# Two blocks in one launch: the steps of S5, its loads and its gate are placed differently, and two norms get idle matmuls

## The chip, the cores and the metric

The kernel runs on one core of one Trainium2 chip. What counts is the time of one execution on the device, in microseconds; the median over runs is given.

## The reference

A sequence of 256 tokens with 2048 features in fp32 goes through two different transformer blocks. What the change touches:

```
first block:   xn = rmsnorm(h);  z = xn @ w_in        -> q, k, v, o, gates, u
               hm = mlstm(q, k, v, gates)             4 heads of 256, chunks of 128 tokens
               ys = s5_groups(u, ...)                 64 groups of 16 channels, state 64 (complex),
                                                      then per group a gated linear unit (s5_glu_w)
               h  = h + concat[hm, ys] @ w_out
               h  = h + peer(rmsnorm(h))              8 heads choose among experts peer_u, peer_v
               x  = rmsnorm(h)
second block:  h = rms_norm(x) * (1 + scale1) + shift1;   x = x + gate1 * mixing_sublayer(h)   (w_in_2, w_out_2)
               h = rms_norm(x) * (1 + scale2) + shift2;   x = x + gate2 * swiglu(h)            (w_ffn_in, w_ffn_out)
```

S5 is a linear recurrence per group. The kernel computes it in pieces of 8 tokens: "taps" are the direct products within a piece, "in" gives each piece's contribution to the state, the recurrence over the 32 pieces gives the states, and "out" adds taps and states to the output. Gelu and the gated linear unit follow.

## The kernel before

All large products run on TensorE as three matmuls per piece of K: an fp32 weight is split into a high and a low part (ScalarE copies it rounded, L247, VectorE subtracts, L248), the activations have been split before (xh, xl), and L274 to L276 multiply high by low, high by high and low by high. A weight chunk (`raw`, 512 KB, loaded by SyncE at L238) holds two pieces of K of 128 rows for 512 columns, so that it is 12 matmuls: two pieces, two halves of the tokens, three products. Four split buffers and four `raw` buffers stand. A tile of 512 columns accumulates in two banks `g` (psG has four), and its callback copies them out.

Everything beside the projections is written as generators in queues (`side`). `gemm` calls `step` after each weight chunk, and `step` advances the first generator of each queue by n steps. The Tile framework then orders the instructions of each engine from the order in which they were traced and from its own simulated times, so that the place of a step in the program sets its rank; it may move ahead or fall back on its engine.

The second half of `w_in` in phase_a has eight tiles of eight chunks, 64 chunks, at two steps per chunk: v, q, k and o of heads 0 and 1, then the same of heads 2 and 3. Beside it run, in queue 0, `s5_all`: put_u (5 steps), taps(1), in(0), taps(2), in(1), taps(3), in(2), in(3) (37 steps), states (15), and for each quarter q out(q) (6), and for q-1 move and gate (8, of which 6 are empty). In queue 1 and 2 run the gates and the heads of the mLSTM; heads 0 and 1 are added when k(2), the third tile, is done (chunk 24). taps(0) runs earlier, in the first half of `w_in`.

Transposes, S5's products and the heads' products take banks `b` of psS, four in all. `in(q)` is a chain of transposes (L308), copies on ScalarE, matmuls (L518), a copy and transposes again. The recurrence (L540 to L543) is 31 times four operations on GpSimd, in order. `out(q)` needs the taps out of DRAM (Kd, L554, tile `s5t0`, one buffer), builds a matrix on VectorE (L563 ff.), multiplies (L576, L582), transposes and applies Gelu. The move (L599, L603) stores the quarter to DRAM in eight pieces and loads it back turned; the gate (L610) multiplies it and puts it into `ys`. When all four are done, `ys` is split (L849, L850) for the second half of w_out's K, which runs first; then `hm`, the heads' output, is transposed and split for the first half.

The q and k tiles are copied by ScalarE (`ev`, L813, two buffers), transposed into banks `b` and convolved. v goes to V1 (L806, one buffer), which heads 0 and 1 hold until they are done; heads 2 and 3 use it next. The output gate `og` has one buffer too.

The first norm (`final_norm` and `norm_T`) stands between the expert products of `peer` (L1115 to L1117) and the second block's `w_in`: the last products' sums are added and transposed (`put_Y`, L308 into banks `g`), the root is found (`rC`, L301), transposed to a row (L308), and VectorE and ScalarE make xh and xl (L346, L348). The second norm is the same between `w_out_2` and `w_ffn_in`.

Of the kernel before, what the change touches and what calls it, by code (L numbers as in the profile page):

```python
# [24 lines left out]
T = 256  # L25
# [125 lines left out]
class Kern:  # L151
    def __init__(self, tc, A, ctx):
        self.tc, self.nc, self.A, self.ctx = tc, tc.nc, A, ctx
        self.side = [[], [], []]
        self.GB, self.heads = {}, set()
        self.raw_slots, self.raw_n = [None], 0
        self.half_step = []

    def pool(self, name, bufs=1, space=None):
# [10 lines left out]
    def step(self, n=1):  # L170
        for q in self.side:
            for _ in range(n):
                while q:
                    try:
                        next(q[0])
                        break
                    except StopIteration:
                        q.pop(0)
# [147 lines left out]
    def norm_r(self, work, ss, name="rstd"):  # L326
# [3 lines left out]
        return self.rstd(work, st, D, name)  # L330

    def put_Y(self, YT, Y, k0, bank=None):

        for k in range(0, Y[0].shape[-1] // 128, 2):
            p = self.transpose4([Y[tb][:, (k + i) * 128:(k + i + 1) * 128] for i in range(2) for tb in range(2)], bank)
            self.nc.scalar.activation(YT[:, k0 + k:k0 + k + 2].rearrange("p k t -> p (k t)"), p, AF.Copy)

    def norm_T(self, YT, r, xh, xl, work, gain, shift):

        nc, V = self.nc, self.nc.vector  # L340
        b = self.transpose4([r[:, tb:tb + 1].to_broadcast([128, 128]) for tb in range(2)])
        row = work.tile([128, T], F32, name="nrow")
        nc.scalar.activation(row, b[:, :T], AF.Copy)
        for k in range(KD):
            v = work.tile([128, T], F32, name="nv", bufs=4)
            V.scalar_tensor_tensor(v, YT[:, k], gain[:, k:k + 1], row, op0=OP.mult, op1=OP.mult)  # L346
            nc.scalar.activation(xh[:, k], v, AF.Identity, bias=shift[:, k:k + 1])
            V.scalar_tensor_tensor(xl[:, k], v, shift[:, k:k + 1], xh[:, k].bitcast(F32), op0=OP.add, op1=OP.subtract)  # L348


    def s5_params(self, p):
        nc = self.nc
        prm = p.tile([128, 96 + 2048], F32, name="s5prm")
        nc.sync.dma_start(prm, self.A["s5p"])
        lre, lim, ldt = (prm[:, i * 32:(i + 1) * 32] for i in range(3))
# [87 lines left out]
    def s5_taps(self, p, q):  # L443
# [37 lines left out]
        dr = self.pb.tile([128, 16, 16], F32, name="t", bufs=3)  # L481
        nc.sync.dma_start(dr.rearrange("p g o -> p (g o)"), self.A["s5d"][:, q * 256:(q + 1) * 256])
        nc.gpsimd.tensor_tensor(dr, dr, self.ident[:, None, :16].to_broadcast([128, 16, 16]), op=OP.mult)
# [47 lines left out]
    def s5_states(self, p):  # L531
# [5 lines left out]
        for c in range(31):  # L537
# [6 lines left out]
            if c % 2:  # L544
                yield

    def s5_out(self, p, q, yg):

        nc, V, q5 = self.nc, self.nc.vector, self.s5
        pw, pn, cn, U, S = q5["pw"], q5["pn"], q5["cn"], self.U[q], self.S  # L550
        ms = slice(8 * q, 8 * q + 8)
        t0 = p.tile([128, 8, 16, 16], F32, name="s5t0")
        k = self.Kd
        nc.sync.dma_start(t0.rearrange("p i g o -> p (i g o)"),  # L554
                            bass.AP(tensor=k.tensor, offset=k.offset + q * 16 * 3840,
                                    ap=[[256, 8], [3840, 16], [1, 2048]]))

# [12 lines left out]
        for hf in range(2):  # L570
# [7 lines left out]
            for a in range(2):  # L578
                for r in range(2):
                    for gr in range(4):  # L580
# [4 lines left out]
                                         tile_position=(hf * 64, gr * 32))  # L585
            nc.scalar.activation(YS[:, hf * 256:(hf + 1) * 256], b[:, :256], AF.Copy)
        yield
        b = self.transpose4([YS[:, i * 128:(i + 1) * 128] for i in range(4)])
        nc.scalar.activation(yg[:, 16 * q:16 * q + 16].rearrange("p g c -> p (g c)"), b, AF.Gelu)
        yield  # L590

    def s5_glu(self, p, q, yg, ys):

        nc, V = self.nc, self.nc.vector
        if q == 0:
# [7 lines left out]
        nc.sync.dma_start(yT, yd[2 * q:2 * q + 2].rearrange("n p x -> p n x"))  # L603
        for _ in range(6):
            yield
        for hf in range(2):
            gt = hf * 4 + q
            b = self.bank()
            for s in range(2):
                nc.tensor.matmul(b[:, s * 256:(s + 1) * 256], self.glu[:, gt, s, :], yT[:, hf],  # L610
                                 start=s == 0, stop=s == 1, skip_group_check=True)
            sg = self.pb.tile([128, 256], F32, name="t", bufs=3)
# [5 lines left out]
    def s5_all(self, p, uT, ys):  # L618
        yield from self.s5_put_u(p, uT)
        self.glu = p.tile([128, 8, 2, 128], F32, name="s5c")  # L620
        self.nc.sync.dma_start(self.glu.rearrange("p a b c -> p (a b c)"), self.A["glu"])
        for q in range(4):
            if q < 3:
                yield from self.s5_taps(p, q + 1)
            yield from self.s5_in(p, q)
        yield from self.s5_states(p)
        yg = self.xx.tile([128, 64, 32], F32, name="X1")
        for q in range(4):
            yield from self.s5_out(p, q, yg)
            if q:  # L630
                yield from self.s5_glu(p, q - 1, yg, ys)
        yield from self.s5_glu(p, 3, yg, ys)

# [112 lines left out]
    def phase_a(self):  # L746
        nc, V, A = self.nc, self.nc.vector, self.A
        with ExitStack() as ex:
# [19 lines left out]
            bg = mp.tile([128, 8], F32, name="bg")  # L768
            nc.sync.dma_start(bg, A["b_gates"])
            self.add_side(self.s5_params(s5))  # L770
# [69 lines left out]
            for tb in range(2):  # L840
                nc.sync.dma_start(X[tb], A["x"][tb * 128:(tb + 1) * 128, :])
            xh = self.act.tile([128, KD, T], F32R, name="xh")
            xl = self.act.tile([128, KD, T], F32R, name="xl")
            mix = [[s5.tile([128, 8, T], F32R, name=n, bufs=2 if n == "s5q" else 1) for n in nn]
                   for nn in (("s5q", "s5q"), ("s5t0", "s5b"))]
            for q in range(4):
                k, y = slice(2 * q, 2 * q + 2), ys[:, 2 * q:2 * q + 2]
                h, l = (z[:, k] for z in mix[1])
                nc.scalar.activation(h, y, AF.Copy)  # L849
                V.tensor_tensor(l, y, h.bitcast(F32), op=OP.subtract)  # L850

# [236 lines left out]
    def peer_v(self, p, AT, half, slots, steps=1):  # L1088
# [44 lines left out]
        for hf in range(2):  # L1133
# [4 lines left out]
            self.step(4 * steps)  # L1138
        more.close()
        self.drain()  # L1140
        return P

    def peer(self, xh, xl, r):
# [37 lines left out]
        def final_norm():  # L1181
# [4 lines left out]
            for n in range(4):  # L1186
                s = slice(n * 512, (n + 1) * 512)
                Y = [p.tile([128, 512], F32, name="fy", bufs=4) for _ in range(2)]
                for tb in range(2):
# [3 lines left out]
                    for z, j in ((x, 0), (Y[tb], 1)):  # L1193
# [4 lines left out]
                        else:  # L1198
                            nc.scalar.activation(sq, z, AF.Square, accum_out=ss[:, j, tb, n:n + 1])
                self.put_Y(YT, Y, 4 * n, self.bank_g)  # L1200
            st = p.tile([128, 2, 2], F32, name="fst")
            V.tensor_reduce(st.rearrange("p a b -> p (a b)"), ss.rearrange("p a b n -> p (a b) n"), axis=AX.X, op=OP.add)
# [329 lines left out]
    def phase_c(self, p, get_x):  # L1532
# [3 lines left out]
        with ExitStack() as ex2:  # L1536
# [3 lines left out]
            xl = self.act.tile([128, KD, T], F32R, name="xl")  # L1540
            self.norm_T(YT, r2, xh, xl, p, gain, shift)
            self.keep.close()
# [130 lines left out]
            with tp(name="po", bufs=1) as p:  # L1673
# [13 lines left out]
                def cb_o(i, P):  # L1687
# [7 lines left out]
                    self.put_Y(YT, [X[tb][:, s] for tb in range(2)], s.start // 128)  # L1695
                self.gemm("w_out_2", LAST, KD, yh, yl, cb_o)
                xh = self.act.tile([128, KD, T], F32R, name="xh")
                xl = self.act.tile([128, KD, T], F32R, name="xl")
                self.norm_T(YT, self.norm_r(p, ss), xh, xl, p, gain, shift)
                for tb in range(2):  # L1700
# [56 lines left out]
```

## Time and profile before

| | us |
|---|---|
| median of 3 runs | 3672.2 (3669.62 to 3672.81) |
| profiled execution | 3670.36 |
| its span, first to last instruction | 3668.6 |
| TensorE busy | 3570.9 (97%) |
| VectorE busy | 2722.6 (74%) |
| ScalarE busy | 2006.5 (55%) |
| GpSimd busy | 542.9 (15%) |
| mean granted TensorE clock | 0.991 |

TensorE is PE in the rows, VectorE DVE, ScalarE ACT, GpSimd POOL, SyncE SP. Matmuls are pipelined, so that the starts of successive ones lie closer than each lasts. The clock is the share of full speed that was granted; its two levels are 1.2 and 2.4 GHz.

### The profile page before, as it was taken

What the parts mean: (1) busy time and instruction counts of PE and PEld (TensorE: products, weight loads), DVE (VectorE), ACT (ScalarE), POOL (GpSimd) and SP (SyncE); (2) the same over time, 40 slices, a digit from 0 to 9 for tenths busy, and PEclk for the clock granted to TensorE, in tenths of its full rate; (3) what the DMA queues carried; (4) which work ended last, traced back from release to release, by engine and by line L of the source; (5) the groups of instructions that cost most, each with busy time, mean ns of one, the idle gap of its engine ahead of it and who ended that gap; (6) DMA issues with size and microseconds to landing.
All of it is one profiled execution on the core that took longest, in us unless ns stands there. A gap on an engine that the chain in (4) does not pass through costs nothing. (4 is left out here: it accounts for less than half of the span.)

```text
span 3668.6 us, 52912 instructions
## 1 busy us (share of the span) xinstructions
PE 3570.9 (97%) x17442; PEld 2957.3 (81%) x17442; DVE 2722.6 (74%) x5631; ACT 2006.5 (55%) x3511; POOL 542.9 (15%) x669
## 2 busy tenths in 40 slices
PE   9997999999999999999999999999999999999999
PEld 7776887788888788887888788888887888888888
DVE  8685779759999977777777878765777666666554
ACT  5555655555555455555555665765455555555443
POOL 1060002204455500001000101000111000000000
PEclk9998999999999999999999999999999999999999
DMA  7656555555555578888887554566886577777665
GB/s 207 185 161 152 186 176 161 167 183 175 171 166 173 166 248 285 288 284 312 290 285 262 180 157 135 160 202 196 281 292 224 165 228 227 235 224 218 189 196 161
DMA packets 228515, 766.07 MB, mean 209 GB/s; under 512 B 40528, under 2 KB 44496, under 8 KB 226192
## 3 DMA queue, kind: packets, MB, share of 16 engines
q1 hardware_dynamic: 197728, 647.89, 56.0%
q0 software_dynamic: 30512, 114.81, 9.9%
q8 instruction: 137, 2.24, 0.2%
q14 instruction: 138, 1.13, 0.1%
HBM read 753.23 MB, written 9.37 MB: 208 GB/s over the span
## 5 line engine op out<-in xcount | busy, mean ns | idle before, releaser
L247 ACT ACTIVATE wh<-raw 128x512 fp32r<-128x512 f32 (+2 forms) x2068 | 1287.9, 628 | 1285.8 <-PE g L275 638.3
L248 DVE TENSOR_TENSOR wl<-raw,wh 128x512 fp32r<-128x512 f32 (+2 forms) x2068 | 1453.8, 713 | 670.3 <-ACT wh L247 621.0
L274 PE MATMUL g<-wh,xl 128*128 128x512 f32 (+2 forms) x3296 | 1271.6, 386 | 14.4 <-ACT wh L247 9.2
L275 PE MATMUL g<-wh,xh 128*128 128x512 f32 (+2 forms) x3296 | 1265.4, 384 | 0.0
L276 PE MATMUL g<-wl,xh 128*128 128x512 f32 (+2 forms) x3296 | 1096.7, 387 | 27.4 <-DVE wl L248 27.3
L276 PEld LDWEIGHTS g<-wl,xh 128*128 128x128 f32 x3296 | 611.7, 189 | 152.8 <-DVE wl L248 41.4
L274 PEld LDWEIGHTS g<-wh,xl 128*128 128x128 f32 x3296 | 623.7, 189 | 136.1 <-ACT wh L247 10.9
L275 PEld LDWEIGHTS g<-wh,xh 128*128 128x128 f32 x3296 | 623.5, 189 | 118.0 <-issue 0.4
L1115 PE MATMUL g<-wh,uev 128*128 128x512 f32 x504 | 196.5, 390 | 3.7 <-ACT wh L247 2.2
L1115 PE MATMUL b<-wh,uev 128*128 128x512 f32 x504 | 196.2, 389 | 0.0
L1116 PE MATMUL g<-wh,uev 128*128 128x512 f32 x504 | 196.1, 389 | 0.0
L1116 PE MATMUL b<-wh,uev 128*128 128x512 f32 x504 | 196.1, 389 | 0.0
L248 DVE TENSOR_TENSOR wl<-xh,wh 128x512 fp32r<-128x512 f32 x202 | 135.3, 688 | 68.7 <-ACT wh L247 27.9
L1057 POOL TENSOR_TENSOR e<-e,t 128x256 fp32r<-128x256 f32 x128 | 131.0, 1027 | 367.6 <-DVE e L1056 272.4
L247 ACT ACTIVATE wh<-xh 128x512 fp32r<-128x512 f32 x202 | 127.6, 632 | 51.6 <-PE g L1116 38.3
L274 PE MATMUL g<-wh,fl 128*128 128x512 f32 (+1 forms) x440 | 154.4, 351 | 0.0
L275 PE MATMUL g<-wh,fh 128*128 128x512 f32 (+1 forms) x440 | 154.2, 351 | 0.0
L910 POOL DMA_DIRECT2D xl<-in_w_ada x116 | 61.2, 528 | 595.2 <-DVE xl L906 585.8
L1117 PE MATMUL g<-wl,uev 128*128 128x512 f32 x504 | 147.5, 389 | 0.9 <-DVE wl L248 0.9
L906 DVE SCALAR_TENSOR_TENSOR xl<-xl 128x1024 f32<-128x1024 f32 x116 | 141.5, 1220 | 8.2 <-DMA xl<-in_w_ada 8.2
L1117 PE MATMUL b<-wl,uev 128*128 128x512 f32 x504 | 146.9, 390 | 0.0
L276 PE MATMUL g<-wl,fh 128*128 128x512 f32 (+1 forms) x440 | 132.6, 348 | 0.0
(558 smaller groups left out, 4111.6 us busy)
## 6 DMA issues: line engine op xcount, KB each, us to landing
raw<-in_peer_u SPq DMA_DIRECT2D x256, 512.0 KB, 3.6
raw<-in_w_in SPq DMA_DIRECT2D x192, 512.0 KB, 3.6
raw<-in_w_ffn_in SPq DMA_DIRECT2D x176, 512.0 KB, 4.2
raw<-in_peer_v SPq DMA_DIRECT2D x130, 512.0 KB, 5.6
xl<-in_w_ada POOLq DMA_DIRECT2D x116, 512.0 KB, 5.9
xh<-in_peer_v SPq DMA_DIRECT2D x101, 512.0 KB, 5.3
raw<-in_w_ffn_out SPq DMA_DIRECT2D x88, 512.0 KB, 4.1
raw<-in_w_out SPq DMA_DIRECT2D x64, 512.0 KB, 4.1
```

Of the source, the lines that this page charges most:

```text
L247: nc.scalar.activation(h[:, :n], r, AF.Copy)
L248: nc.vector.tensor_tensor(l[:, :n], r, h[:, :n].bitcast(F32), op=OP.subtract)
L274: nc.tensor.matmul(o, xl[:, k - ka, t], hs, start=k == ka, stop=False)
L275: nc.tensor.matmul(o, xh[:, k - ka, t], hs, start=False, stop=False)
L276: nc.tensor.matmul(o, xh[:, k - ka, t], ls, start=False, stop=k == kb - 1)
L906: self.tc.keep_in_program_order(nc.vector.scalar_tensor_tensor(r, r, 1.0, cr, op0=OP.mult, op1=OP.mult, accum_out=self.macc[:, 2 * m + hf: ...
L910: nc.gpsimd.dma_start(r, w[n * 128:(n + 1) * 128, cs])
L1057: E.tensor_tensor(o2[:, :, 1], f(o2[:, :, 0]), bc(f(self.wl), t), op=OP.mult)
L1115: nc.tensor.matmul(o, w[:, 1, t], h, start=i1 == 0, stop=False)
L1116: nc.tensor.matmul(o, w[:, 0, t], h, start=False, stop=False)
L1117: nc.tensor.matmul(o, w[:, 0, t], l, start=False, stop=i1 == 127)
```

## The change

While S5's taps and inputs run, queue 0 advances three steps per chunk instead of two (`dense`). The load of the taps for a quarter is issued at the end of the quarter before, ahead of its transposes (`s5_load`), and for the first quarter ahead of the states. The move of quarter q comes right behind out(q), and its gate behind out(q+1) with no empty steps between; its matmuls are kept in the order of the program. The split of `ys` for w_out moves into `s5_all`: quarters 0 to 2 ahead of ten empty steps and the last gate, quarter 3 behind it. The loads of S5's parameters, of its diagonal and of the gate bias go from SyncE's queue to GpSimd's. Matmuls whose result is never read (`fill`) are put in: 10 each after the last two quarters of `final_norm`, 8 in its `norm_T`, 16 after `w_out_2` and 8 in the `norm_T` that follows.

```diff
 def step(self, n=1):
         for q in self.side:
-            for _ in range(n):
+            for _ in range(n + (self.dense if q is self.side[0] else 0)):
...
+    def fill(self, l, r, n):
+
+        b = self.bank()
+        for _ in range(n):
+            self.nc.tensor.matmul(b, l, r, start=True, stop=True)
...
-    def norm_T(self, YT, r, xh, xl, work, gain, shift):
+    def norm_T(self, YT, r, xh, xl, work, gain, shift, fill):
...
         nc.scalar.activation(row, b[:, :T], AF.Copy)
+        fill()
...
-        nc.sync.dma_start(prm, self.A["s5p"])
+        nc.gpsimd.dma_start(prm, self.A["s5p"])
...
-        nc.sync.dma_start(dr.rearrange("p g o -> p (g o)"), self.A["s5d"][:, q * 256:(q + 1) * 256])
+        nc.gpsimd.dma_start(dr.rearrange("p g o -> p (g o)"), self.A["s5d"][:, q * 256:(q + 1) * 256])
...
+    def s5_load(self, p, q):
+
+        self.t0 = p.tile([128, 8, 16, 16], F32, name="s5t0")
+        k = self.Kd
+        self.nc.sync.dma_start(self.t0.rearrange("p i g o -> p (i g o)"),
+                               bass.AP(tensor=k.tensor, offset=k.offset + q * 16 * 3840,
+                                       ap=[[256, 8], [3840, 16], [1, 2048]]))
...
     def s5_out(self, p, q, yg):
...
+        t0 = self.t0
...
+        if q < 3:
+            self.s5_load(p, q + 1)
         yield
         b = self.transpose4([YS[:, i * 128:(i + 1) * 128] for i in range(4)])
...
-    def s5_glu(self, p, q, yg, ys):
+    def s5_move(self, q, yg):
...
         nc.sync.dma_start(yT, yd[2 * q:2 * q + 2].rearrange("n p x -> p n x"))
-        for _ in range(6):
-            yield
+        return yT
+
+    def s5_glu(self, q, yT, ys):
...
-                nc.tensor.matmul(b[:, s * 256:(s + 1) * 256], self.glu[:, gt, s, :], yT[:, hf],
-                                 start=s == 0, stop=s == 1, skip_group_check=True)
+                self.tc.keep_in_program_order(
+                    nc.tensor.matmul(b[:, s * 256:(s + 1) * 256], self.glu[:, gt, s, :], yT[:, hf],
+                                     start=s == 0, stop=s == 1, skip_group_check=True))
...
+        self.dense = 1
         for q in range(4):
             if q < 3:
                 yield from self.s5_taps(p, q + 1)
             yield from self.s5_in(p, q)
+        self.dense = 0
+        self.s5_load(p, 0)
         yield from self.s5_states(p)
         yg = self.xx.tile([128, 64, 32], F32, name="X1")
+        yT = None
         for q in range(4):
             yield from self.s5_out(p, q, yg)
             if q:
-                yield from self.s5_glu(p, q - 1, yg, ys)
-        yield from self.s5_glu(p, 3, yg, ys)
+                yield from self.s5_glu(q - 1, yT, ys)
+            yT = self.s5_move(q, yg)
+        self.mix_s5(p, ys, (0, 1, 2))
+        for _ in range(10):
+            yield
+        yield from self.s5_glu(3, yT, ys)
+        self.mix_s5(p, ys, (3,))
+
+    def mix_s5(self, p, ys, qs):
+
+        if qs[0] == 0:
+            self.ysh, self.ysl = (p.tile([128, 8, T], F32R, name=n) for n in ("s5t0", "s5b"))
+        for k in [4 * hf + q for hf in range(2) for q in qs]:
+            self.nc.scalar.activation(self.ysh[:, k], ys[:, k], AF.Copy)
+            self.nc.vector.tensor_tensor(self.ysl[:, k], ys[:, k], self.ysh[:, k].bitcast(F32), op=OP.subtract)
...
-            nc.sync.dma_start(bg, A["b_gates"])
+            nc.gpsimd.dma_start(bg, A["b_gates"])
...
+        self.filler = ws[127][:, 0, 0:128], ws[127].rearrange("p a t -> p (a t)")
         self.drain()
         return P
...
                 self.put_Y(YT, Y, 4 * n, self.bank_g)
+                if n > 1:
+                    self.fill(*self.filler, 10)
...
-            self.norm_T(YT, r2, xh, xl, p, gain, shift)
+            self.norm_T(YT, r2, xh, xl, p, gain, shift, lambda: self.fill(*self.filler, 8))
...
                 self.gemm("w_out_2", LAST, KD, yh, yl, cb_o)
+                filler = p.tile([128, 512], F32R, name="fill")
+                nc.scalar.activation(filler, yh[:, 0:2], AF.Copy)
+                self.fill(filler[:, 0:128], filler, 16)
...
-                self.norm_T(YT, self.norm_r(p, ss), xh, xl, p, gain, shift)
+                self.norm_T(YT, self.norm_r(p, ss), xh, xl, p, gain, shift,
+                            lambda: self.fill(filler[:, 0:128], filler, 8))
```

## Rows read from the trace of the kernel before

**Rows 1.** Busy time by stage: stretch, us, busy and instructions of each engine, clock, DMA share, GB/s.
```profile
277.00:351.00 74.00, 55.03 (x448) 42.14 (x448) 42.22 (x75) 39.14 (x63) 0.00 (x0) 0.82 0.65 155
351.00:397.00 46.00, 46.00 (x213) 37.76 (x212) 33.30 (x105) 24.27 (x52) 0.00 (x0) 1.00 0.50 155
...
2041.00:2058.00 17.00, 9.95 (x39) 7.43 (x38) 15.29 (x46) 10.82 (x25) 1.14 (x2) 0.70 0.50 186
...
2913.50:2928.00 14.50, 7.89 (x24) 5.62 (x23) 12.22 (x38) 8.06 (x19) 0.00 (x0) 0.65 0.20 69
...
sum 3668.60, PE 3570.87 PEld 2957.33 DVE 2722.56 ACT 2006.51 POOL 542.93; mean PE 357.09 PEld 295.73 DVE 272.26 ACT 200.65 POOL 54.29
```

**Rows 2.** Timeline of TensorE, 277 to 351 us; in brackets the idle time before and its releaser.
```profile
321.40 0.65 PE L576 MATMUL b<-s5t,X 128*32 128x128 f32 x16 [3.13 <-DMA s5t<-Kd]
...
330.52 3.53 PE L610 MATMUL b<-e,s5c 128*128 128x256 f32 x8 [3.38 <-DMA e<-yd]
...
345.01 0.79 PE L274 MATMUL g<-wh,s5b 128*128 128x512 f32 x1 [4.50 <-DVE s5b L850]
```

**Rows 3.** Busy time and count of L274 on TensorE from the span's start to three times.
```profile
0.00:129.10 129.10, 57.37 (x160) 0.97 0.72 207
0.00:199.50 199.50, 88.60 (x238) 0.98 0.67 192
...
0.00:267.40 267.40, 120.88 (x320) 0.99 0.64 185
```

**Rows 4.** Timeline of TensorE, transposes and S5 output matmuls that use banks b.
```profile
146.84 0.60 PE L308 MATMUL b<-ident,e 128*128 128x128 f32 x4
147.27 1.04 PE L308 MATMUL b<-ident,ev 128*128 128x128 f32 x8
...
199.63 0.60 PE L308 MATMUL b<-ident,e 128*128 128x128 f32 x4
200.07 1.04 PE L308 MATMUL b<-ident,ev 128*128 128x128 f32 x8
...
267.51 0.64 PE L576 MATMUL b<-s5t,X 128*32 128x128 f32 x16
```

**Rows 5.** Timeline of GpSimd: the first and the last operation of the recurrence that waited or ended.
```profile
202.87 0.32 POOL L542 TENSOR_TENSOR s5t<-s5t,X 128x64 f32<-128x64 f32 x1 [51.32 <-DVE X L528]
...
267.34 0.72 POOL L543 TENSOR_TENSOR s5b<-s5t,s5t 128x64 f32<-128x64 f32 x1
```

**Rows 6.** Timeline of TensorE, matmuls of 512 columns at full clock; three lie between.
```profile
92.15 0.39 PE L275 MATMUL g<-wh,xh 128*128 128x512 f32 x1
...
93.06 0.39 PE L276 MATMUL g<-wl,xh 128*128 128x512 f32 x1
```

**Rows 7.** SyncE's issues of two lines: count, ns min/median/max, first and last start.
```profile
L554 SPq DMA_DIRECT2D s5t<-Kd x4: 604/627/648, 156.9 to 306.9; - x4
...
L599 SPq DMA_DIRECT2D yd<-X x32: 302/448/3194, 279.0 to 333.4; - x32
```

**Rows 8.** Timeline of TensorE at the first norm.
```profile
2029.42 0.71 PE L308 MATMUL g<-ident,AT 128*128 128x128 f32 x5
...
2040.72 1.58 PE L308 MATMUL g<-ident,AT 128*128 128x128 f32 x13
...
2051.32 0.79 PE L274 MATMUL g<-wh,xl 128*128 128x512 f32 x1 [2.58 <-DVE xl L348]
```

**Rows 9.** Timeline of TensorE at the second norm.
```profile
2918.78 0.66 PE L308 MATMUL b<-ident,rstd 128*128 128x128 f32 x2 [2.51 <-DVE rstd L301]
...
2922.01 0.80 PE L274 MATMUL g<-wh,xl 128*128 128x512 f32 x1 [2.58 <-DVE xl L348]
```

**Rows 10.** Timeline of TensorE where the first half of w_out ends.
```profile
397.52 1.47 PE L308 MATMUL b<-ident,hm 128*128 128x128 f32 x12
```

**Rows 11.** Timeline of ScalarE, two copies out of the projection's accumulators.
```profile
128.94 0.69 ACT L813 ACTIVATE ev<-g,rA 128x512 f32<-128x512 f32 x1 [0.28 <-PE g L276]
...
266.75 1.27 ACT L806 ACTIVATE V<-g,rA 128x512 f32<-128x512 f32 x2 [0.27 <-PE b L723]
```

More of the change, by code (lines that the diff above doesn't have):

```diff
@@ L551, in s5_out @@
         ms = slice(8 * q, 8 * q + 8)
[L552 to L556, printed above, removed]
+        t0 = self.t0
         G2 = p.tile([128, 2, 8, 8, 16], F32, name="s5q", bufs=2)
@@ L590, in s5_out @@
         yield
-    def s5_glu(self, p, q, yg, ys):
-        nc, V = self.nc, self.nc.vector
+    def s5_move(self, q, yg):
+        nc = self.nc
         if q == 0:
@@ L603, in s5_glu @@
         nc.sync.dma_start(yT, yd[2 * q:2 * q + 2].rearrange("n p x -> p n x"))
-        for _ in range(6):
-            yield
+        return yT
+    def s5_glu(self, q, yT, ys):
+        nc, V = self.nc, self.nc.vector
         for hf in range(2):
@@ L625, in s5_all @@
             yield from self.s5_in(p, q)
+        self.dense = 0
+        self.s5_load(p, 0)
         yield from self.s5_states(p)
         yg = self.xx.tile([128, 64, 32], F32, name="X1")
+        yT = None
         for q in range(4):
@@ L843, in phase_a @@
             xl = self.act.tile([128, KD, T], F32R, name="xl")
[L844 to L850, printed above, removed]
+            mix = [[s5.tile([128, 8, T], F32R, name="s5q", bufs=2) for _ in range(2)], [self.ysh, self.ysl]]
             def mix_hm():
```

## The prediction

> **What bounds the kernel now.** I read the busy shares by stage first. TensorE is busy 3570.87 of 3668.60 us [rows 1], so the sum of all its gaps is 97.7 us, and an edit can only win where TensorE stands still or runs below full clock. Three of the stages there have such gaps and are touched by the diff. From 277 to 351 us TensorE is busy 55.03 of 74.00 us, so 18.97 us are idle, and its granted clock is 0.82; that it lies between the two levels means that it spent part of the stretch at 1.2 GHz, and 55.03 x (1 - 0.82) = 9.9 us is what that costs. From 2041 to 2058 (the first norm) it is busy 9.95 of 17 at 0.70, and from 2913.5 to 2928 (the second) 7.89 of 14.5 at 0.65. The stretch right behind the first, 351 to 397, is full: 46.00 of 46.00 us at 1.00.
>
> Next I read TensorE's timeline of 277 to 351. Seven waits make up the 18.97 us; [rows 2] has three of the larger ones. All belong to S5: its output matmuls (L576), its gate (L610), and the first w_out product, which waits 4.50 us for the split of S5's result (L850).. So S5's tail is late, and the projection's matmuls have run out by then.
>
> Why it is late is seen by following S5 back. Counting L274 on TensorE [rows 3] (four per weight chunk, 96 before the second half of w_in) shows that at 129.1 us 16 chunks were done, at 199.5 us 35.5, at 267.4 us 56. The last input transposes run just then, at 199.63 us [rows 4], although the generator puts them at chunk 21.5. The recurrence on GpSimd starts 3 us later and runs until 268.06 us, 65 us in all [rows 5], and out(0) follows at 267.51 [rows 4]. Behind it come four times out, move, gate.
>
> **The change part by part.** A chunk is 12 matmuls; four at full clock take 93.06 - 92.15 = 0.91 us [rows 6], so one is 0.2275 us and a chunk 2.73 us.
>
> *Three steps per chunk.* Taps 1 to 3 and the four inputs are 37 steps: 18.5 chunks at two per chunk, 12.3 at three. The recurrence is placed 6.2 chunks earlier, or 16.8 us. That is the upper bound of the gain. The lower bound is nothing: S5 runs 14 chunks behind its place already (35.5 against 21.5), since each of its TensorE groups waits for a copy of the one before and products that are ready go ahead meanwhile. Neither end fits by itself: being traced earlier gives each step an earlier turn, but does not shorten a round trip. I take the middle, 8.4 us.
>
> *What such a gain is worth.* Nothing of the tail disappears; what moves 8.4 us earlier are its waits, and products still to do fill them. Idle 18.97 and clock 9.9 make 28.8 us that could be won at most, so 8.4 fits within it. The recurrence's own 65 us stay.
>
> *Move and gate, taps a quarter ahead.* The load of Kd (L554) was issued for the last time at 306.9 us [rows 7], after the last L576 of the quarter before, and out(3) starts at 321.40 after waiting 3.13 us for it [rows 2]. The new place in the program is earlier, but the buffer is single: the load still cannot start before that L576 has read it, and SP issues it as soon as it has. I cost it at nothing, with a gain of 3.13 us as the upper bound. The move (8 stores of yd and a reload) is traced one out earlier and the gate loses its six empty steps. The stores are 32 of 0.448 us [rows 7]; nine issues a quarter are some 4 us of SP, and weight loads queue behind them. They began at 279.0 us, right behind out(0), so SP runs them by readiness already and their place changes nothing. The reload's wait of 3.38 us [rows 2] is the bound on either side: out's work covers it or the next one has it. The pin keeps the gate's matmuls behind the instruction traced before them; they run later than their place already, so nothing. The splits of quarters 0 to 2 come ahead of the last gate, so two of eight pairs remain behind it; the 4.50 us of the last wait [rows 2] bound the gain, and I leave it in the 8.4. Queued behind a late gate on TensorE are the transposes of q and k of the second half, and behind them heads 2 and 3.
>
> *Loads moved from SP to GpSimd* (the S5 parameters, four diagonals, the gate bias): six DMAs of the same bytes. Taps and inputs end before the recurrence, and GpSimd stood idle for 51.32 us ahead of it [rows 5]; that is the cover, and I cost the move at nothing. Without it, one issue costs 0.63 us of a queue (L554 in [rows 7]), six 3.8.
>
> *Idle matmuls at the first norm.* 10 after each of n = 2 and 3, 8 in the norm: 28 x 0.2275 = 6.4 us of TensorE. Full clock in 2041 to 2058 would give 9.95 x 0.30 = 3.0 us. Against it, the transposes of the output are run among the products as soon as they are ready, from 2029.42 us [rows 8], 11 us before the last ones at 2040.72. Fills that follow in the program can be put there as well, and 20 of them delay the products by up to 4.5 us. The 8 others (1.8 us) fit into the 2.58 us ahead of the first product at 2051.32 [rows 8]. Gain 3.0, loss 4.5; the rows do not say which, and I take 0.
>
> The Trainium skill ("TensorE: Matmul & The Clock Gate", Part 2: What happens when you issue a matmul) speaks against them: only weight loads are pulled ahead, matmuls stay in program order, so a fill ahead of a ready product is paid in full. By it the sum is 4.5 us worse wherever the fills are placed as the transposes at 2029.42 are; no run here has shown a fill yet.
>
> *Idle matmuls at the second norm.* 16 after the last product, 8 in the norm. TensorE waits 2.51 us ahead of 2918.78 and 2.58 us ahead of 2922.01 [rows 9]. The 16 take 3.64 us and are shorter than the stretch from 2913.5 to 2918.78; the 8 take 1.8 of 2.58. So they cost nothing, and full clock would give 7.89 x 0.35 = 2.8 us. I take 2.7, as the fills start a little into the stretch. If the clock falls anyway: 0. If all 52 fills of both norms were paid: 11.8 us lost.
>
> **Sum.** 3670.36 (the profiled execution) - 8.4 - 0 - 2.7 = 3659.3 us. That execution is 1.8 us below the median of the runs (3672.2), so 3661 us as a median.
>
> **The rivals.**
>
> *A: the tail gains nothing (same).* The round trips of the inputs, not the steps, set their pace, or what S5 gains is lost at heads 2 and 3. For it: the lag of 14 chunks [rows 3]; and that the transposes of `hm`, which need the last head, start at 397.52 with no wait ahead of them [rows 10], right behind a stretch in which TensorE was full [rows 1]: the heads come just in time. If they do not get earlier, 397.5 stays and the gain turns into a wait there. Against it: the accumulator banks of the side work are handed out in program order, and the transposes of k(2) wait for in(3) (200.07 behind 199.63 [rows 4]), so that earlier inputs also bring k earlier. Only the second norm's 2.7 are left: 3672.2 - 2.7 = 3669.5.
>
> *B: heads 0 and 1 fall behind the recurrence (slower).* Twelve chunks of steps instead of 18.5 bring out(0) to chunk 26, where heads 0 and 1 (added at chunk 24, with two empty steps) ask for banks. Banks go out in the order of the program: q(1)'s transposes come right behind in(1)'s, 147.27 behind 146.84, though their copy was done at 128.94 + 0.69 [rows 4, 11]. If out(0) is ahead of the heads, they wait for the recurrence. V1 is single, so v(4) keeps its accumulators until the heads are done: today ACT copies it at 266.75 [rows 11], and 56 chunks are done by 267.4 [rows 3], so og(7) gets its accumulators with no slack. From then on each microsecond that the heads are later is one lost. Heads ran from k(2)'s transposes, 200.07, to 266.75, 67 us; if half of that came after the recurrence (268 - 8), they would end 33 us later than now, and if none, at the same time. The middle, 16 us, against the gain elsewhere of 2.7: 3672.2 + 16 - 2.7 = 3685.5. Against it: heads 0 and 1 start at chunk 24, two chunks ahead of out(0), and step at the same pace.
>
> *C: the fills of the first norm are paid (same).* The 20 land among the products, as the transposes at 2029.42 do [rows 8], and the products end 4.5 us later: 3661 + 4.5 = 3665.5. Against it: a fill has no data to be ready for, and may come last as well. This is what the rule above would do.
>
> *D: the whole tail is won.* If move and taps also find their data, all 28.8 us go: 3672.2 - 28.8 - 2.7 = 3641.
>
> **How the numbers follow.** About 0.2%, 7.3 us, is what a measurement of this kernel can tell from no change. My forecast (3661, itself 3655 to 3665) has a chance of 0.38, A 0.24, B 0.21, C 0.10, D 0.07. Forecast and D are faster, 0.45; A and C are the same, 0.34; B is slower, 0.21. The range reaches from 3644, most of the way to D, to 3684, most of the way to B; it leaves out half of B and of D, 0.14. All fills paid with nothing won in the tail (3672.2 + 11.8 = 3684.0) is its upper end too.
>
> **What would show it.** Right: GpSimd's recurrence starts at about 193 instead of 202.87; the wait ahead of the first w_out product after the S5 split ends at about 337 instead of 345; the clock of the second norm's stretch is near 1.00 and its 14.5 us are about 12. A is seen when the recurrence starts within 3 us of 202.87, or when a wait ahead of the `hm` transposes appears near 390. B is seen when V1's copy lies after out(0) and TensorE stands idle at about chunk 56. The first norm is read from the last product's end: later than 2040.7, relative to the stage's start, if fills were put in front. The prediction is wrong if a queue that I cost at nothing, GpSimd's loads or SP's order, delays a weight chunk.

## The result and the profile after

The changed kernel takes 3693.59 us (median of 4 runs, 3693.24 to 3695.13) against 3672.34 before: 21 us slower, ratio 1.0060 with an interval of 1.0043 to 1.0078. The profiled execution took 3693.24 us, its span is 3691.2 us. The forecast of 3661 was wrong, and 3693.6 lies above the range's end of 3684. What came is the order of rival B (3685.5), heads 0 and 1 behind the recurrence, and a time above its forecast.

TensorE's timeline of the changed kernel, its S5 and head instructions (L309, L588, L594, L751 and L628 are L308, L576, L582, L716 and L610 of before):

```profile
193.01 0.60 PE L309 MATMUL b<-ident,e 128*128 128x128 f32 x4
193.45 1.04 PE L309 MATMUL b<-ident,ev 128*128 128x128 f32 x8
...
200.36 1.08 PE L588 MATMUL b<-s5t,X 128*32 128x128 f32 x32
259.19 2.98 PE L594 MATMUL b<-s5q,s5b 64*32 64x128 f32 x64 [12.97 <-POOL s5b L551]
...
265.52 0.38 PE L309 MATMUL b<-ident,kT 128*128 128x128 f32 x2
...
297.84 0.65 PE L588 MATMUL b<-s5t,X 128*32 128x128 f32 x16
...
357.79 1.97 PE L628 MATMUL b<-e,s5c 128*128 128x256 f32 x8 [1.40 <-DMA e<-yd]
...
361.11 0.66 PE L309 MATMUL b<-ident,ev 128*128 128x128 f32 x4 [0.48 <-ACT ev L848]
...
385.63 0.38 PE L309 MATMUL b<-ident,kT 128*128 128x128 f32 x2
```

The inputs end at 193.01 instead of 199.63 us [rows 4], and q's transposes, which stood behind in(1) at 147.27, now stand behind in(3) at 193.45. Out(0)'s direct products run at 200.36. Its state products are then next on TensorE and wait 12.97 us for the last operation of the recurrence. Only behind them come the k transposes of heads 0 and 1, at 265.52 us; and out(1), which followed out(0) by 15 us before (267.51 and 282.69), starts at 297.84, behind the heads.

GpSimd's recurrence, ScalarE's last step of k and its copy of V1, and VectorE's last splits of weights ahead of the wait:

```profile
195.94 0.32 POOL L550 TENSOR_TENSOR s5t<-s5t,X 128x64 f32<-128x64 f32 x1 [44.97 <-DVE X L536]
...
258.82 0.32 POOL L551 TENSOR_TENSOR s5b<-s5t,s5t 128x64 f32<-128x64 f32 x1
```

```profile
233.69 1.07 ACT L859 ACTIVATE kT<-kT 128x1024 f32<-128x1024 f32 x1 [0.89 <-DVE kT L857]
...
297.08 1.27 ACT L841 ACTIVATE V<-g,rA 128x512 f32<-128x512 f32 x2
```

```profile
244.66 2.88 DVE L249 TENSOR_TENSOR wl<-raw,wh 128x512 fp32r<-128x512 f32 x4 [4.12 <-PE g L276]
```

The recurrence starts 6.9 us earlier than in [rows 5] and ends 8.9 earlier, as forecast (8.4). But k, ready at 234.76, is not transposed until 265.52, and V1 is copied 30.3 us later than in [rows 11]. The Trainium skill ("TensorE: Matmul & The Clock Gate", Part 2: What happens when you issue a matmul) says that matmuls stay in program order; the trace agrees, since from 246.2 to 259.19 us k's transposes, ready since 234.76, and products whose weights were split by 247.54 stood behind a matmul that had nothing to work on until 259.1. L275 counted from the start (as in [rows 3]) says what the projections did meanwhile:

```profile
0.00:246.00 246.00, 110.66 (x296) 0.99 0.67 191
0.00:259.10 259.10, 110.66 (x296) 0.97 0.65 186
0.00:283.70 283.70, 120.69 (x320) 0.96 0.62 179
0.00:302.40 302.40, 120.69 (x320) 0.95 0.59 172
```

No product of a weight chunk runs from 246.0 to 259.1 us, at chunk (296 - 96) / 4 = 50, and none from 283.7 to 302.4, at chunk 56. This standstill, and V1's copy behind out(0), are the signs that the prediction named for rival B. The stages after that, of which the first has more left to do than before (55.03 us busy in [rows 1]) and the second is no longer full:

```profile
277.00:351.00 74.00, 60.71 (x480) 46.94 (x478) 40.48 (x133) 37.43 (x78) 0.10 (x1) 0.86 0.55 146
351.00:397.00 46.00, 43.19 (x196) 34.74 (x197) 34.59 (x67) 26.98 (x48) 0.00 (x0) 1.00 0.57 179
```

The `hm` transposes come at 421.37 us instead of 397.52 [rows 10], 23.9 later. Between there and the end 1.3 us are won (3691.2 - 421.37 = 3269.8 against 3668.6 - 397.52 = 3271.1). So all of the loss is in S5 and the heads.

At the norms the idle matmuls (L337) did what they were to do. The first norm, then the second:

```profile
2066.10 0.62 PE L1146 MATMUL b<-wl,e 128*128 128x512 f32 x2
...
2068.13 4.59 PE L337 MATMUL b<-e 128*128 128x512 f32 x19
...
2074.08 2.08 PE L337 MATMUL b<-e 128*128 128x512 f32 x8
2076.90 0.50 PE L275 MATMUL g<-wh,xl 128*128 128x512 f32 x1 [0.74 <-DVE xl L356]
```

```profile
2940.50 3.92 PE L337 MATMUL b<-fill 128*128 128x512 f32 x16
...
2944.72 2.09 PE L337 MATMUL b<-fill 128*128 128x512 f32 x8
2947.81 0.50 PE L275 MATMUL g<-wh,xl 128*128 128x512 f32 x1 [1.00 <-DVE xl L356]
```

```profile
2066.50:2083.50 17.00, 15.97 (x81) 12.93 (x80) 15.54 (x45) 11.25 (x25) 1.14 (x2) 1.00 0.54 189
2939.20:2953.70 14.50, 12.52 (x59) 9.93 (x58) 12.00 (x38) 8.46 (x20) 0.00 (x0) 1.00 0.21 71
```

All 20 of the first norm stand behind the last product at 2066.10, and the clock is 1.00 in stretches that had 0.70 and 0.65 [rows 1]. What this gives lies behind the norm: at the second one the stretch from the last product to the next is no shorter (8.63 us against 8.40), but in the first 5 us of products behind it the kernel before runs 12 matmuls at a clock of 0.50, the lower level, and the changed one 22 at 1.00:

```profile
2922.01:2927.01 5.00, 5.00 (x12) 0.50 0.00 0
```

```profile
2947.81:2952.81 5.00, 5.00 (x22) 1.00 0.00 0
```

### The profile page after: what moved, and what is told of

The parts are those of the page before. It is cut to its first block, busy times and chain, and to the rows that moved or that the text cites. A ratio compares the mean times of both kernels' runs of the same rounds, so it can differ in the third digit from the quotient of the medians.

```text
span 3691.2 us, 53035 instructions
## 1 busy us (share of the span) xinstructions
PE 3586.0 (97%) x17494; PEld 2968.6 (80%) x17494; DVE 2717.8 (74%) x5635; ACT 2005.6 (54%) x3513; POOL 547.6 (15%) x675
## 5 line engine op out<-in xcount | busy, mean ns | idle before, releaser
L275 PE MATMUL g<-wh,xl 128*128 128x512 f32 (+2 forms) x3296 | 1270.1, 386 | 11.0 <-ACT wh L248 7.1
L277 PE MATMUL g<-wl,xh 128*128 128x512 f32 (+2 forms) x3296 | 1095.5, 387 | 27.6 <-DVE wl L249 27.5
L277 PEld LDWEIGHTS g<-wl,xh 128*128 128x128 f32 x3296 | 610.7, 189 | 152.9 <-DVE wl L249 42.1
L275 PEld LDWEIGHTS g<-wh,xl 128*128 128x128 f32 x3296 | 622.8, 189 | 132.5 <-ACT wh L248 7.9
L1086 POOL TENSOR_TENSOR e<-e,t 128x256 fp32r<-128x256 f32 x128 | 128.9, 1011 | 363.9 <-DVE e L1085 271.0
L275 PE MATMUL g<-wh,fl 128*128 128x512 f32 (+1 forms) x440 | 154.4, 351 | 0.0
L277 PE MATMUL g<-wl,fh 128*128 128x512 f32 (+1 forms) x440 | 132.7, 348 | 0.0
```

Source lines behind the costliest of these rows:

```text
L275: nc.tensor.matmul(o, xl[:, k - ka, t], hs, start=k == ka, stop=False)
L277: nc.tensor.matmul(o, xh[:, k - ka, t], ls, start=False, stop=k == kb - 1)
L1086: E.tensor_tensor(o2[:, :, 1], f(o2[:, :, 0]), bc(f(self.wl), t), op=OP.mult)
```

## The experiments

The theory that I set against the others is called order: heads 0 and 1 used to run in the shadow of the 65 us of the recurrence; with three steps the first output quarter is put ahead of them on TensorE, whose matmuls wait in line, so that they run behind the recurrence, on the chain that ends with `hm`. The rivals are the gate (its new place costs the time) and what else the early inputs move. Each run stands against the kernel before on its own chip:

| run | median | before | ratio and interval | `hm` at |
|---|---|---|---|---|
| the change | 3693.59 | 3672.34 | 1.0060 (1.0043 to 1.0078) | 421.37 |
| e1_two_steps | 3673.30 | 3670.52 | 1.0008 (0.9998 to 1.0018) | 398.92 |
| e2_only_dense | 3685.49 | 3670.52 | 1.0045 (1.0029 to 1.0062) | 415.55 |
| e3_heads_first | 3673.79 | 3670.52 | 1.0014 (1.0004 to 1.0023) | 402.94 |
| e4_no_fill | 3695.22 | 3670.52 | 1.0076 (1.0059 to 1.0093) | 419.67 |
| e5_only_fill | 3665.26 | 3666.91 | 0.9997 (0.9988 to 1.0006) | 395.70 |
| e6_only_gate | 3671.08 | 3666.91 | 1.0011 (1.0002 to 1.0020) | 399.60 |
| e7_second_v1 | 3700.03 | 3666.91 | 1.0089 (1.0074 to 1.0103) | 433.89 |
| e8_taps_ahead | 3649.75 | 3666.91 | 0.9961 (0.9948 to 0.9973) | 374.51 |
| e12_order_only | 3686.99 | 3670.23 | 1.0049 (1.0033 to 1.0064) | 415.80 |
| e9_taps_gate | 3653.89 | 3670.23 | 0.9951 (0.9937 to 0.9964) | 385.87 |
| e10_taps_dense | 3672.20 | 3670.23 | 1.0006 (0.9996 to 1.0015) | 402.67 |
| e11_taps_nofill | 3659.87 | 3670.23 | 0.9968 (0.9956 to 0.9980) | 381.46 |
| x1_taps_fill | 3656.21 | 3670.00 | 0.9958 (0.9944 to 0.9972) | 380.79 |
| x2_taps_nofill | 3658.30 | 3670.00 | 0.9970 (0.9959 to 0.9982) | 373.11 |
| x3_taps_gate | 3651.55 | 3670.00 | 0.9954 (0.9941 to 0.9968) | 383.32 |

Three kernels were run twice, on different chips: e8 and x1, e9 and x3, and e11 and x2 are the same. Their traces differ by up to 8.4 us in `hm` (381.46 and 373.11), so that a smaller difference in `hm` alone says little.

**The three steps, undone.**

```diff
-        self.dense = 1
+        self.dense = 0
```

> The changed kernel, but S5's taps and inputs advance two steps per chunk as before; all else of the change stays. Theory (order): the whole loss of some 24 us up to the transposes of hm comes from the three steps, which put the first quarter's output products ahead of heads 0 and 1 on TensorE, so that TensorE stands before L594 until the recurrence is done. Then this kernel has heads 0 and 1 at their old place (k transposes near 225 us), hm near 397 us, and keeps the 6.0 us that the idle matmuls win at the two norms: 3666 us, 3662 to 3670. Rival (gate): the later gate, its pin and the loads moved to GpSimd cost the time: it stays near 3690 us.

The 3693.6 fall to 3673.3, above the 3662 to 3670 expected, and `hm` comes at 398.92. The order theory holds for the bulk; but the 6 us of the idle matmuls do not show, so the rest of the change costs about what they give.

**The three steps alone**, on the kernel before.

```diff
-            for _ in range(n):
+            for _ in range(n + (self.dense if q is self.side[0] else 0)):
...
+        self.dense = 1
         for q in range(4):
             if q < 3:
                 yield from self.s5_taps(p, q + 1)
             yield from self.s5_in(p, q)
+        self.dense = 0
```

> The kernel before with the three steps per chunk alone. Theory (order): TensorE waits about 13 us ahead of the first quarter's state products, heads 0 and 1 start near 265 us, hm near 421 us, and without the idle matmuls the time is 3672 + 24 = 3696 us, 3692 to 3701. Rival (gate): three steps alone only bring S5 earlier: 3672 us or less.

1.0045, or 16.5 us: the wait and the late heads are there, `hm` is 18 us late. The theory had put all 24 us on the three steps; some 7 were too many.

**All of the change, heads first.**

```diff
+        while not {0, 1} <= self.heads:
+            yield
         for q in range(4):
             yield from self.s5_out(p, q, yg)
```

> The changed kernel with all its parts, three steps too, but the first output step of S5 is held back in the program until heads 0 and 1 have been traced. Theory (order): the recurrence keeps its early start (about 196 us), heads come ahead of the output products again, hm is near 397 us and the time 3666 us, 3660 to 3671; the q and k convolutions are still late behind in(3), which may take back some us. Rival (gate): no difference to the changed kernel, 3690 us or more. Second rival (the early inputs themselves, q's transposes behind in(3), cost the time): 3680 us or more.

TensorE no longer waits ahead of the state products, and V1 is copied at 270.01 us:

```profile
270.01 1.26 ACT L843 ACTIVATE V<-g,rA 128x512 f32<-128x512 f32 x2 [1.17 <-PE b L760]
```

Of the 1.0060 1.0014 is left, and the time lies above the 3660 to 3671 expected. The inputs' early end, which this kernel keeps, shows no gain: its heads start at 237.50 us instead of 224.81, because q waited for in(3), and out(0) now waits for the heads (272.59 against 268.11).

**The order alone**: the kernel before with two steps, heads 0 and 1 held back until out(0) has been traced.

```diff
         for _ in range(2):
             yield
+        while h < 2 and not self.out0:
+            yield
```

> The kernel before, two steps per chunk, nothing of the change; only heads 0 and 1 are held back in the program until the first output step of S5 has been traced, so that their order on TensorE is that of the changed kernel. Theory (order): this alone costs what the three steps cost: TensorE waits 10 us or more ahead of the first state products, V1 is copied 25 to 35 us later than 267, hm lies 15 to 25 us later than 397, and the time is 3685 us, 12 to 25 above the kernel before on the same chip. Rival (the three steps cost by what else they move, such as q's transposes behind in(3)): within 6 us of the kernel before.

```profile
264.66 2.99 PE L583 MATMUL b<-s5q,s5b 64*32 64x128 f32 x64 [10.89 <-POOL s5b L544]
...
415.80 1.47 PE L309 MATMUL b<-ident,hm 128*128 128x128 f32 x12
```

1.0049 with no third step anywhere: a wait of 10.89 us at the same place, V1 at 297.56 and `hm` at 415.80, against 415.55 with three steps alone. The order of out(0) and the heads is the cause, and the three steps only brought it about.

**A second buffer for V1**, on the changed kernel (the first half of S5's parameters gets a tile of its own, which V1 of the second half uses later).

```diff
-                    V1 = cur[0] = mp.tile([128, 2, 2, 257], F32, name="V1")
+                    V1 = cur[0] = (s5 if half else mp).tile([128, 2, 2, 257], F32, name="s5pa" if half else "V1")
```

> The changed kernel with a second buffer for V1 (in the place of parameters that taps no longer need), so that v of the second half leaves its accumulators at chunk 40 and og can start at chunk 56. Rival B as it stood (accumulators held): TensorE's standstill at chunk 56, 283 to 305 us, is filled and the time falls by 10 to 20 us: 3677 us. Theory (chain): the heads lie between out(0) and out(1) on the chain that ends with hm; products done earlier only leave a wait later: hm within 5 us of 421, 3688 to 3694 us.

Rival B had the accumulators that v holds as the price. They are free here, all 64 chunks are done by 327 us (352 of L277), and the kernel is slower still, 1.0089. What came in their place is seen on TensorE between the heads' first k transposes and out(1): busy time and count of L275 (four per chunk), first in the changed kernel, then in this one; then out(1), and the load behind it on SyncE's queue:

```profile
265.52:297.84 32.32, 8.20 (x21) 3.95 (x21) 0.89 0.36 115
```

```profile
268.85:313.09 44.24, 20.00 (x51) 9.59 (x51) 1.00 0.55 167
```

```profile
313.09 0.65 PE L590 MATMUL b<-s5t,X 128*32 128x128 f32 x16
...
314.83 0.64 PE L590 MATMUL b<-s5t,X 128*32 128x128 f32 x16
```

```profile
315.54 0.62 SPq L561 DMA_DIRECT2D s5t<-Kd  x1
```

The projection runs ahead, and (51 - 21) x 3 = 90 more of its matmuls stand among the steps of the heads: from their first transposes to out(1) it takes 44.2 us instead of 32.3, and out(1) starts 15 us later. The load of the taps of out(2) goes out at 315.54, right behind out(1)'s last read of the single buffer (300.33 in the changed kernel, likewise), so that the quarters behind it are late too. I had expected `hm` to stay where it was, and it came 12.5 us later. So the chain through S5 and the heads sets `hm`, not TensorE's room; what the held accumulators alone cost, this run does not say.

**The idle matmuls**, left out of the change (`fill` returns at once), and alone on the kernel before.

> The changed kernel without the idle matmuls; nothing else differs. If they win 3.0 us at each norm, as the distances in the trace of the changed kernel say: 3693.6 + 6.0 = 3699.6 us, 3697 to 3702. If they are paid in front of products: 3690 or less. If they do nothing: 3693.6.

> The kernel before with the 52 idle matmuls alone. If they lie behind the last products and keep the clock at its upper level, each norm gives 2.5 to 3.0 us back: 5 to 6 us less than the kernel before on the same chip, 3665 us. If they lie in front of products (the rule of program order decides): 3 to 5 us more, 3675. If nothing: 3670.5.

Left out: 1.0076 against 1.0060, intervals that overlap. Alone: 0.9997, not to be told from nothing, where I had expected 5 to 6 us. L274 counted from the first product behind the first norm, first with them alone, then in the kernel before:

```profile
2049.62:2149.62 100.00, 59.90 (x172) 1.00 0.62 190
...
2049.62:2349.62 300.00, 148.95 (x402) 0.98 0.52 158
```

```profile
2051.32:2151.32 100.00, 59.74 (x168) 0.97 0.60 188
...
2051.32:2351.32 300.00, 149.47 (x402) 0.98 0.51 157
```

After 100 us the kernel with them is 4 ahead, 12 matmuls or 2.7 us; after 300 us both stand at 402. The lead of the first norm is gone by then in this pair. Over all traces, from the first product behind the first norm to the first behind the second, the ten with idle matmuls take 867.5 to 871.4 us (mean 869.9) and the seven without 868.6 to 875.1 (871.0), so less than half of the 2.7 is kept in the mean, within the spread. From the second norm's first product to the end the ten take 743.4 to 744.3 (743.7) and the seven 744.9 to 746.6 (745.5): 1.8 us, and no overlap. Together some 3 us.

**The move and the gate alone**: two steps, no idle matmuls, loads on SyncE.

> The kernel before with the move, the gate, the taps' load and the split of ys as in the change, but two steps, no idle matmuls and the loads on SyncE. What two steps with all else of the change left (3.3 us over the kernel before, with idle matmuls worth 6) says: 6 to 9 us slower, 3678 us, because the last gate comes ahead of the transposes of q and k of the second half and so of heads 2 and 3: k transposes later than 352, hm at 400 or later. Rival (that loss is a chance of weight loads elsewhere): no slower than 2 us, hm at 397.

1.0011, some 4 us, in the expected direction and less than the 6 to 9 expected. The last gate comes at 344.26, ahead of the k transposes of the second half, and heads 2 and 3 start from 363.70 (352.14 before):

```profile
344.26 1.97 PE L626 MATMUL b<-e,s5c 128*128 128x256 f32 x8 [1.78 <-DMA e<-yd]
346.06 1.04 PE L309 MATMUL b<-ident,ev 128*128 128x128 f32 x8
363.70 0.38 PE L309 MATMUL b<-ident,kT 128*128 128x128 f32 x2
```

In the changed kernel the same place of the gate holds q back as well: q and k are transposed from 359.6 to 363.9, the heads start at 385.63 and `hm` is 5.8 us later than with three steps alone (421.37 against 415.55). That the gate's place is what costs the 4 us is argued from these lines: in both kernels `hm` moves by less than two traces of one kernel can differ (here 399.60 against 397.52). e1 differs from this run only by the idle matmuls and the loads on GpSimd, and its `hm` lies at 398.92, so the moved loads do not show.

**The taps' loads in halves**, on the kernel before with the idle matmuls. The idea was that each of the tail's quarters waits for a load that a single buffer keeps back; here a quarter's load is two halves in three buffers. The halves and the buffers are not separated, nor the tiles that had to move to make room.

```diff
-        t0 = p.tile([128, 8, 16, 16], F32, name="s5t0")
+        t0 = [p.tile([128, 8, 8, 16], F32, name="s5h", bufs=3) for _ in range(2)]
```

> The kernel before with the idle matmuls and with the taps' loads cut into halves in three buffers (parameters split in two tiles to make room), so that each quarter's load goes out a half ahead of its use; two steps per chunk, gate and move as before. If each quarter of S5's tail waits for its load (12 to 14 us from issue to use), the tail of 77 us shrinks by 10 to 25 us and the time is 3650 us, 3640 to 3660. Rival (move, gate and heads 2 and 3 set the end): no more than the idle matmuls give, 3665 us.

0.9961: 3649.75 us, faster than both kernels. TensorE's timeline, out(0), out(1), out(3) and `hm`:

```profile
263.43 0.64 PE L589 MATMUL b<-s5h,X 128*32 128x128 f32 x16
...
267.39 0.64 PE L589 MATMUL b<-s5h,X 128*32 128x128 f32 x16
...
305.15 0.64 PE L589 MATMUL b<-s5h,X 128*32 128x128 f32 x16
...
374.51 1.04 PE L308 MATMUL b<-ident,hm 128*128 128x128 f32 x8
```

The kernel before: the load for out(1), and out(1); then out(1) with the idle matmuls alone, on the chip of this run:

```profile
269.99 0.62 SPq L554 DMA_DIRECT2D s5t<-Kd  x1
```

```profile
282.69 1.08 PE L576 MATMUL b<-s5t,X 128*32 128x128 f32 x16 [4.55 <-DVE ml_r L301]
```

```profile
282.36 0.87 PE L583 MATMUL b<-s5t,X 128*32 128x128 f32 x16 [4.38 <-DMA s5t<-Kd]
```

out(3) starts 16 us earlier than in [rows 2], and `hm` 23 us earlier than in [rows 10]. But only one load's way was won, that of out(1): it follows out(0) by 4.0 us, where it was 15.2 (267.51 [rows 4] and 282.69), and the other five traces with halves and two steps have 3.9 to 4.0 as well. From out(1) to out(3) it is 37.8 us, against 38.7 before, so the loads behind it were not what those quarters waited for. The load of out(1) went out behind out(0)'s last read of the buffer and was used 12.7 us later, yet its wait shows as 4.4 to 4.6 us, since other products filled the rest. The 3.13 us that I read in [rows 2] was the wait of out(3). Another 4 us lie ahead of out(0) (263.43 against 267.51); what brings them stays open.

**Three steps on top of that.**

> The taps' loads in halves and the idle matmuls with three steps per chunk; gate and move as before. Theory (order): out(0) lies ahead of heads 0 and 1 again, TensorE waits 10 us or more for the recurrence, hm lies 15 to 25 us behind 374: 3662 to 3675. Rival (three steps lose by the late loads of taps in S5's tail, which are gone here): 3650 or less.

1.0006 against 0.9961 without them (on another chip), 16.5 us again, with 10.05 us of wait ahead of the state products. So the loss does not come from the loads of the tail.

**The gate on top of that, and the idle matmuls taken off it**, first on one chip, then on another beside the kernel that they start from.

> The taps' loads in halves and the idle matmuls, as in the run before, and the move and gate placed as in the change (no empty steps, ten ahead of the last gate, no pin). If the last gate's place ahead of k's transposes of the second half is what cost the gate's part its 4 us: k transposes near 345 instead of 330, hm 380 to 390 instead of 374, 3655 to 3662 us. Rival (the gate's place is free, and the 9 us that TensorE waited ahead of the last gate are now covered): 3641 to 3648.

> The taps' loads in halves without the idle matmuls. If the idle matmuls give 2.7 us (the second norm's alone, since the lead of the first was lost 300 us later in the trace with them alone): 3652.5 us. If both norms give 3: 3656. If they give nothing: 3649.8.

> The taps' loads in halves with the idle matmuls, again, beside the same kernel without idle matmuls and the same with the change's gate on one chip. 0.4% faster than the kernel before, 14 us.

> Without the idle matmuls: if only the second norm keeps its gain, 2.7 us more than with them; if both norms do, 5.5 to 6; if none, equal.

> With the idle matmuls and the change's move and gate. If the last gate ahead of k's transposes costs here what the trace shows (hm at 386 instead of 375): 5 to 11 us more than with the gate as before. If it is free: within 2 us.

Side by side: 0.9958 with idle matmuls, 0.9970 without, 0.9954 with the gate of the change. The intervals overlap. The idle matmuls are worth 2 to 4 us by these numbers, not clear of zero, and with taps ahead the gate's place costs nothing that can be seen, although `hm` came at 385.87 and 383.32 in its traces, against 374.51 and 380.79 without: the expectation of 5 to 11 us failed. From `hm` to the end the traces with the gate of the change take 3268.8 and 3270.6 us and those without 3272.4 and 3273.6, so part of an earlier `hm` is lost again behind it; where, no run here shows.

## Why the prediction was wrong

- **What bounds the kernel** held: the loss and the one real gain found (taps ahead) both lie between 200 and 400 us.
- **Three steps per chunk** held in itself: the recurrence starts 6.9 us earlier and ends 8.9 earlier, 8.4 forecast.
- **"What such a gain is worth" failed**: I moved the tail's waits earlier by the same amount and forgot what stood in the recurrence's shadow. The heads were there, 224.81 to 266.75 us. Rival B had the place, and I gave it 0.21 for a reason that is the failed step, as written: "heads 0 and 1 start at chunk 24, two chunks ahead of out(0), and step at the same pace". Counted in the kernel's steps they are not ahead. With three steps out(0)'s products are traced in chunk 26 (32 before), and k's transposes, behind the two empty steps of the heads, in chunk 26 too; `step` advances queue 0 first, so out(0) has the earlier rank. Its direct products ran at 200.36 us, while k waited for q, and q for in(3); its state products were placed at chunk 50, ahead of the heads, and TensorE stood 12.97 us. Why the framework did not place them later is not shown.
- **Rival B's price** was the middle of 0 and 33, 16 us; its order alone measured 15 to 18 (e2 and e12, by medians and ratios). That the two agree is luck. The 33 is a slip, since 260 + 33.5 lies 27 us behind 266.75, which makes the middle 13; and the price was argued by the accumulators that V1 holds. TensorE did stand at chunk 56, but with these freed the kernel got slower (e7). What the runs show in its place is that the heads lie on the chain, and out(1) behind them.
- **Taps a quarter ahead**, costed at nothing, was right: with two steps and the load's new place (e1) out(1) still waits 4.82 us for it. The bound of 3.13 us was wrong. It is the wait of out(3); the largest of the seven waits, 4.55 us ahead of out(1), hid a load that was worth 11 us there (e8).
- **Move and gate** I put at nothing: some 4 us of loss alone (e6); whether it is more in the changed kernel, where `hm` is 5.8 us later than with three steps alone, is not shown. I had named the queue, q and k behind a late gate, and not priced it.
- **The first norm** I took at 0 between a gain of 3.0 and a loss of 4.5. The fills were placed behind the last product, so rival C did not come and no product was delayed; 2.7 us were won there, of which less than half was kept to the second norm. **The second norm**: 2.7 forecast, 1.8 measured over the traces.
- **Sum**: 16.5 (three steps, e2) + 4 (gate, e6) - 3 (both norms) = 17.5 of the 21.3 measured; the intervals of e2 and of the change reach 6 us either way, so the rest is within them. The loads moved to GpSimd and the pin were not tried by themselves.

## What to carry to other kernels

When a step is brought forward on an engine that runs in order, look at what ran in the shadow of the long operation that it waits for: that work will stand behind it unless it is ready first. Count the ranks with every empty step and with the order in which the queues are advanced; a lead of two chunks was none here. Before moving steps, follow each load of a serial tail from its issue to its use, the first one too: a single buffer that kept one load back showed 4 to 5 us of wait, gave back 11 when it went, and was worth more than all the steps moved here. A stretch freed on the busiest engine is worth nothing if what it lets run ahead gets between the steps of the chain.

## What the runs showed of the hardware

The recurrence's speed depends on whether VectorE works. While VectorE stands idle, from 247.54 to 262.21 us in the changed kernel, a step of four operations on GpSimd takes 1.35 us:

```profile
255.18 0.32 POOL L548 TENSOR_TENSOR s5t<-a8r,s5b 128x64 f32<-128x64 f32 x1
...
256.53 0.32 POOL L548 TENSOR_TENSOR s5t<-a8r,s5b 128x64 f32<-128x64 f32 x1
```

Over the whole recurrence in the same trace, 195.94 to 259.14, the mean is 63.2 / 31 = 2.04 us. That it is VectorE is seen around its four splits, 244.66 to 247.54:

```profile
244.48 0.32 POOL L549 TENSOR_TENSOR s5t<-s5pn,s5b 128x64 f32<-128x64 f32 x1
244.75 0.78 POOL L550 TENSOR_TENSOR s5t<-s5t,X 128x64 f32<-128x64 f32 x1
...
246.95 0.76 POOL L549 TENSOR_TENSOR s5t<-s5pn,s5b 128x64 f32<-128x64 f32 x1
247.68 0.31 POOL L550 TENSOR_TENSOR s5t<-s5t,X 128x64 f32<-128x64 f32 x1
```

TensorE works until 246.2 and ScalarE from 243.99 to 246.66; GpSimd is fast while both work and VectorE does not (244.48), and slow while VectorE alone works (246.95). In what way the two hinder each other, no run here separates.
